# Where the weights' parts and the activations' parts begin in on-chip memory: other offsets, modulo 256 bytes, between the two operands of the large matrix products

## The chip, the cores and the metric

The kernel runs on one core of one Trainium2 chip. Its time is the device time of one execution in microseconds. Three runs of the kernel before took 2641.08, 2643.85 and 2647.0 us; the median, 2643.85 us, is the time that the change is measured against. One further execution was profiled.

## The reference

The reference is two transformer blocks one behind the other on a sequence of 256 tokens of width 1024, all in float32. What matters here are its large products, `x @ W` with 256 rows in `x`:

```python
x = x + 0.5 * swiglu(rms_norm(x, ...), w_gate, w_up, w_down)      # width 2816, twice
u = rms_norm(x, mix_norm) @ w_in ...; x = x + concat([a_out, b_out]) @ w_out
for i in range(2):                                                # two layers
    y = ssd_mixer(hn, ...) if i == 0 else retention(hn, ...)
    h = h + y
    h = h + peer_ffn(rms_norm_2(h, ffn_norm[i]), peer_w_q[i], peer_keys[i], peer_u[i], peer_v[i])
    g = sigmoid(rms_norm_2(h, ple_norm[i]) @ ple_gate[i]); h = h + g * (p[i] @ ple_proj[i])

def peer_ffn(h, w_q, sub_keys, u, v):        # 16384 experts, of which each token uses 8 x 16
    ...                                      # idx, gate: top 16 of the keys' products, per head
    hid = gelu(einsum('tkd,td->tk', u[idx], x))
    return einsum('tk,tkd->td', gate * hid, v[idx])
```

## The kernel before

**Products in parts.** Every large float32 product is made of three products of a reduced type (`fp32r`). The weights `w` and the activations are each split in two parts: the high part is a rounded copy (ScalarE), the low part is what the rounding left (VectorE). `mm3` (L321 to L325) then issues three matrix products into one accumulator: high by high (L323), high by low (L324), low by high (L325). For each of them TensorE first loads a 128x128 stationary operand (PEld in the profile), then streams the moving operand past it (PE).

**Units.** All weights come as 856 units of up to 128 x 1024 floats, in one fixed list (`units`, L1308). The class `Stream` brings them in: `load` starts the DMA of a unit into one of three buffers `w`; `part` makes the parts `wh` (ScalarE, L258) and `wl` (VectorE, L260) in one of three buffers each, and in some stages in one or two lent buffers more; `next` hands a unit's parts to a stage and lets `part` run a few units ahead. A buffer of parts is free again when TensorE has done the last product that reads it. TensorE runs all products in the order in which they are written.

**Two kinds of product.** In nearly all stages the weights' part is the stationary operand and 256 tokens of an activation's part are the moving one (`fm_unit`, L330, and the like): 24 products of 256 columns to a unit. So it is in the two feed-forward blocks, the mixers, the experts' first half, and the gates at the end of each layer. The experts' first half takes 128 units of `peer_u` per layer (in `peer`, L1067), in each of which the inner products of 128 experts with 256 tokens are made; beside them VectorE runs the routing (`route`, side work handed out by `Side.run`, some 1.5 us a unit) and then the building of the gates (`gated`). In the experts' second half, 128 units of `peer_v` per layer, the activation's part (the gated `hid`) is stationary and 512 columns of a weights' part move: 12 products of 512 columns to a unit, with the rest of the gates built beside its first 64 units. The values of the mixers (`w_mv`, `w_uv`, `ret_v`) are also of this second kind.

**Where the operands begin.** The built program gives each buffer a fixed address. Of the two operands of a product, the first byte of each within a partition, modulo 256, is what the change is about:

- All buffers of weights' parts begin at 64 modulo 256, the lent ones too, and pieces of 128 columns lie 512 bytes apart, so every piece of a unit has the same remainder. In the `peer_u` units alone, unit k begins 4 x (k mod 64) bytes further on (`self.ws.at`, L1377; `ROOM` is 64 floats).
- All activations' parts that take part in 256-column products begin at 0 modulo 256.
- In the experts' second half the activations' parts of the experts 4b to 4b+3 begin 4 x (4b mod 64) bytes into their buffer (`part_tiles`, L1167), so at 16b modulo 256, and the weights' parts at 64.

Taken as the activations' remainder less the weights' remainder, modulo 256, this makes

| products | offset before |
|---|---|
| 256 columns, all stages but `peer_u` | 192 |
| 256 columns, `peer_u` unit k | 192 - 4 (k mod 64): each multiple of 4 occurs in two units of each layer |
| 512 columns, experts 4b to 4b+3 | 16b - 64: each multiple of 16 occurs in two groups of four experts in each layer |
| 512 columns, values of the mixers | 192 |

In `peer_u`, unit k = 3 has the offset 180, and k = 5 the offset 172; in the experts' second half the offset is 0 for b = 4 and b = 20.

Of the kernel before, what the change touches and what calls it, by code (L numbers as in the profile page):

```python
# [22 lines left out]
FR = mybir.dt.float32r  # L23
# [8 lines left out]
P = 128  # L32
# [3 lines left out]
KC = D // P  # L36
# [8 lines left out]
PK, PH, PT = 128, 8, 16  # L45
UNIT = 1024
# [169 lines left out]


ROOM = 64


class Stream:
# [3 lines left out]
    def __init__(self, nc, wpool, hpool, units, w_bufs, ahead):  # L225
        self.nc, self.wpool, self.hpool = nc, wpool, hpool
        self.units, self.w_bufs, self.ahead = units, w_bufs, ahead
        self.loaded = self.parted = self.given = 0
        self.w, self.parts = {}, {}
        self.pool_every = 0  # L230
        self.spare, self.spares, self.until = None, 0, 0
        self.at = {}

    def lend(self, pool, n, until):

# [10 lines left out]
    def part(self):  # L246
        if self.parted < len(self.units):
            while self.loaded <= self.parted:
                self.load()
            nc, n = self.nc, self.units[self.parted][1]  # L250
            w = self.w.pop(self.parted)
            lent = self.parted < self.until and self.parted % (3 + self.spares) >= 3
            pool = self.spare if lent else self.hpool
            i = self.at.get(self.parted, 0)
            room = UNIT if lent else UNIT + ROOM
            h = pool.tile([P, room], FR, tag="wh", name="wh")[:, i:i + UNIT]
            l = pool.tile([P, room], FR, tag="wl", name="wl")[:, i:i + UNIT]
            nc.scalar.copy(h[:, :n], w[:, :n])  # L258
            own = self.pool_every and self.parted % self.pool_every == 0
            (nc.gpsimd if own else nc.vector).tensor_tensor(l[:, :n], w[:, :n], h[:, :n].bitcast(FT), OP.subtract)  # L260
            self.parts[self.parted] = (h, l)
            self.parted += 1
            while self.loaded < min(self.parted + self.w_bufs, len(self.units)):
                self.load()
# [46 lines left out]
class Program:  # L311
# [25 lines left out]
    def part_tiles(self, at=0):  # L337

        a = self.xpool.tile([P, 8 * S + ROOM], FR, tag="ah", name="ah")[:, at:at + 8 * S]
        return [a[:, k:k + 4 * S].rearrange("p (c t) -> p c t", c=4) for k in (0, 4 * S)]  # L340
# [299 lines left out]
    def mixer(self, r, ready):  # L640
        nc, ws = self.nc, self.ws
        with ExitStack() as ctx:
# [121 lines left out]
            for d in range(3):  # L764
                for _ in range(3):
                    next(mla, None)
                part(d, 4)
            for _ in mla:
                pass
            for d in range(3):  # L770
                part(d, 0)
                self.residual(d, ps[d], ready)
# [294 lines left out]
    def peer(self, l, r, g, ready):  # L1067
        nc, ws = self.nc, self.ws
        with ExitStack() as ctx:
            pool = ctx.enter_context(self.tc.tile_pool(name="peer", bufs=1))  # L1070
# [56 lines left out]
            for b in range(PK // 2):  # L1127
# [11 lines left out]
                if b == PK // 4:  # L1139
                    side.finish()  # L1140
                    scratch.close()
                    pool = ctx.enter_context(self.tc.tile_pool(name="peer2", bufs=1))
# [17 lines left out]
            for e in range(PK):  # L1160
                b, j = divmod(e, 4)
                if e == PK // 2:
                    side.finish()
                    gates.close()
                    self.lend(ws.given + PK - e, 1, ctx)
                if j == 0:
                    ah, al = self.part_tiles(4 * b % ROOM)  # L1167
                    c = 4 * b % (PK // 2)
                    self.split(ah, al, G[2 * e // PK][:, c:c + 4, :])
                group.append((e, ws.next(UNIT), ah[:, j, :], al[:, j, :]))  # L1170
                if e == PK - 2:
                    continue
                if e == PK - 1:
                    self.new_parts()
                for k in range(2):
                    w = slice(512 * k, 512 * k + 512)
                    for t in range(NT):
                        o = slice(t * P, (t + 1) * P)
                        for i, (wh, wl), h, lo in group:
                            self.mm3(acc[t][k], h[:, o], lo[:, o], wh[:, w], wl[:, w], i == 0, i == PK - 1)  # L1180
                    if e == PK - 1:
                        self.features(acc, k, G[0], ready)
                group = []
                side.run(1.2)
# [123 lines left out]
    def units(self):  # L1308
        def rows(name, lo=0, hi=None):
            ap = self.a[name]  # L1310
            out = []
            for u in range(lo, ap.shape[0] if hi is None else hi):
                n = ap.shape[2]
                out += [(ap[u][:, c:min(c + UNIT, n)], min(UNIT, n - c)) for c in range(0, n, UNIT)]
            return out

        def halves(name):
            u = rows(name)
            out = []
            for d0 in range(0, KC, 4):  # L1320
                some = range(d0, d0 + 4)
                out += [u[2 * d + c] for c in range(2) for d in some]
            return out

        self.peer_at = []
        u = rows("ffn1_gu") + rows("ffn1_dn")
        u += rows("w_in", 0, 8) + rows("w_mv") + rows("w_in", 8) + rows("w_kr") + rows("w_uq") + rows("w_uk") + rows("w_uv")
        u += [(self.a["w_out"][d][:, c:c + 512], 512) for c in (512, 0) for d in range(3)] + rows("w_out", 3)
        u += rows("ffn2_gu") + rows("ffn2_dn")
        for l in range(2):  # L1330
            if l == 0:
                u += rows("ssd_in", 0, 1) + rows("ssd_dt") + rows("ssd_in", 1) + halves("ssd_out")
            else:
                for h in range(RET_H):
                    for n in ("ret_qk", "ret_v", "ret_g"):
                        u += rows(n, 4 * h, 4 * h + 4)
                u += halves("ret_out")
            self.peer_at.append(len(u))
            u += rows(f"peer_q{l}") + rows(f"peer_u{l}") + rows(f"peer_v{l}")
            u += rows(f"ple_p{l}") + rows(f"ple_g{l}")  # L1340
        return u

# [22 lines left out]
    def run(self):  # L1365
        nc, tc = self.nc, self.tc
        with ExitStack() as ctx:
# [6 lines left out]
            self.ps2 = None  # L1374
            ctx.callback(lambda: self.ps2 and self.ps2.close())
            self.ws = Stream(nc, wpool, hpool, self.units(), 3, 2)
            self.ws.at = {n + KC * 2 + k: k % ROOM for n in self.peer_at for k in range(PK)}  # L1377

            self.x = consts.tile([P, KC, S], FT, name="x")
            for c in range(0, KC, 2):  # L1380
# [56 lines left out]
            pool = more.enter_context(tc.tile_pool(name="both", bufs=1))  # L1437
# [17 lines left out]
            for l in range(2):  # L1455
# [18 lines left out]
                if l == 0:  # L1474
                    more = ExitStack()
                    pool = more.enter_context(tc.tile_pool(name="xparts2", bufs=1))
# [47 lines left out]
```

## Time and profile before

| | us |
|---|---|
| median of three runs | 2643.85 |
| the profiled execution, time | 2648.24 |
| its span, from the first to the last instruction | 2646.4 |
| TensorE busy (PE) in it | 2579.6 |
| VectorE busy (DVE) | 2003.2 |
| ScalarE busy (ACT) | 1338.3 |

The profile is of one execution. A matrix product's duration in it is that of one product through a pipeline: products start closer to one another than they last, so that the start of one to the start of the next is what a product costs in a dense stretch. PE is shown as busy from a product's start to its modelled end. "Idle before" is the time in which an engine did nothing just ahead of an instruction, and an arrow names what ended that wait.

In the order of time the stages of TensorE are: first feed-forward block to 197 us, first mixer to 323 us (its first eight units alike, to 220 us), second feed-forward block to 503 us, second mixer (`ssd`) to 716 us, 16 units of routing queries to 762 us, `peer_u` of layer 0 to 1158 us, `peer_v` to 1543 us, the layer's gate to 1572 us, the retention mixer to 1776 us, queries to 1820 us, then `peer_u` (to 2218 us), `peer_v` (to 2603 us) and gate of layer 1.

### The profile page before, as it was taken

To read this page: it belongs to the slowest core of one execution; us is meant where nothing else is said; L and a number is where in the kernel's file an instruction comes from. 1 tells how busy PE (TensorE), PEld (TensorE's weight loads), DVE (VectorE), ACT (ScalarE), POOL (GpSimd) and SP (SyncE) were. 2 spreads that over 40 slices of the span, in tenths; PEclk is the share of its full clock that TensorE was granted. 3 is DMA by queue.
4 is the path that set the end of the run, shared out by engine and by line. 5 is a ranking of instruction groups with operands and counts; after the bars stand their busy time and mean duration, and the time that the engine had idled before them with its cause. 6 is when DMAs were issued, how large, how long until landed. Compare 5 with 4: busy or idle time off the path is not lost.

```text
span 2646.4 us, 49065 instructions
## 1 busy us (share of the span) xinstructions
PE 2579.6 (97%) x19798; PEld 2387.6 (90%) x19798; DVE 2003.2 (76%) x3473; ACT 1338.3 (51%) x1824; POOL 192.5 (7%) x216
## 2 busy tenths in 40 slices
PE   8999999998999999999999989999999999999996
PEld 8998899988999999988788879999999998878886
DVE  8656776689789988868865566668999886886555
ACT  6445655577554443444444465555444344444444
POOL 2000100100102020000000030010212000000002
PEclk9999999999999999999999989999999999999998
DMA  6664366564465655555566555556565555555662
GB/s 219 193 185 141 119 198 189 170 208 144 132 197 170 197 173 161 165 177 171 173 185 191 190 160 176 168 162 193 177 191 176 161 162 176 172 171 187 191 189 94
DMA packets 128037, 460.20 MB, mean 174 GB/s; under 512 B 14688, under 2 KB 15424, under 8 KB 127168
## 3 DMA queue, kind: packets, MB, share of 16 engines
q1 hardware_dynamic: 125984, 452.32, 54.9%
q0 software_dynamic: 1536, 4.20, 0.5%
q8 instruction: 155, 2.54, 0.4%
q10 hardware_dynamic: 288, 0.53, 0.1%
q14 instruction: 74, 0.61, 0.1%
HBM read 455.91 MB, written 1.08 MB: 173 GB/s over the span
## 4 chain that ended last, share of the span: by engine, by line
PE 89%; DVE 7%; ACT 2%; issue 1%; DMA 1%; POOL 0%; POOLq 0%; DVEq 0%; ACTq 0%
PE mm L323 18%; PE mm L324 18%; PE mm L325 18%; PE acc L324 9%; PE acc L323 9%; PE acc L325 9%; PE mm L1119 2%; DVE wl L260 2%; DVE eq L1248 1%; DVE f L1251 1%; PE pv L324 1%; PE pv L325 1%; PE sc L1218 1%; PE pv L323 1%; DVE ca L841 0%
## 5 line engine op out<-in xcount | busy, mean ns | idle before, releaser
L258 ACT CAST wh<-w 128x1024 fp32r<-128x1024 f32 x856 | 889.5, 1041 | 1180.3 <-PE mm L324 579.3
L260 DVE TENSOR_TENSOR wl<-w,wh 128x1024 fp32r<-128x1024 f32 x856 | 1045.9, 1223 | 453.3 <-ACT wh L258 451.5
L323 PE MATMUL mm<-ah,wh 128*128 128x256 f32 x3448 | 976.0, 283 | 22.2 <-DVE cv L837 13.7
L325 PE MATMUL mm<-ah,wl 128*128 128x256 f32 x3448 | 970.9, 282 | 6.4 <-DVE wl L260 6.0
L324 PE MATMUL mm<-ah,wh 128*128 128x256 f32 x3448 | 972.2, 282 | 0.0
L323 PEld LDWEIGHTS mm<-ah,wh 128*128 128x128 f32 x3448 | 653.6, 190 | 25.3 <-issue 7.4
L325 PEld LDWEIGHTS mm<-ah,wl 128*128 128x128 f32 x3448 | 651.5, 189 | 11.0 <-DVE wl L260 9.7
L324 PEld LDWEIGHTS mm<-ah,wh 128*128 128x128 f32 x3448 | 652.5, 189 | 0.8 <-issue 0.3
L324 PE MATMUL acc<-wl,ah 128*128 128x512 f32 x1024 | 406.8, 398 | 0.0
L325 PE MATMUL acc<-wh,ah 128*128 128x512 f32 x1024 | 402.4, 394 | 0.0
L323 PE MATMUL acc<-wh,ah 128*128 128x512 f32 x1024 | 369.9, 395 | 0.0
L323 PEld LDWEIGHTS acc<-wh,ah 128*128 128x128 f32 x1024 | 192.5, 188 | 44.0
L325 PEld LDWEIGHTS acc<-wh,ah 128*128 128x128 f32 x1024 | 192.5, 188 | 42.5
L324 PEld LDWEIGHTS acc<-wl,ah 128*128 128x128 f32 x1024 | 192.7, 188 | 42.0
L373 POOL TENSOR_TENSOR sqa<-sqa,sqt 128x256 f32<-128x256 f32 x82 | 81.9, 998 | 1147.0 <-ACT sqt L372 1020.0
L1123 DVE TENSOR_TENSOR G<-mm,G 128x512 f32<-128x512 f32 x128 | 87.9, 688 | 55.4 <-PE mm L1119 54.9
L323 PE MATMUL mm<-hh,wh 128*128 128x256 f32 x352 | 98.0, 278 | 0.0
L324 PE MATMUL mm<-hl,wh 128*128 128x256 f32 x352 | 98.0, 278 | 0.0
L325 PE MATMUL mm<-hh,wl 128*128 128x256 f32 x352 | 98.0, 278 | 0.0
L1119 PEld LDWEIGHTS <-two 128*128 128x128 f16 x2048 | 69.6, 97 | 21.2 <-issue 16.4
L1107 DVE TENSOR_TENSOR two<-iota,tabs 128x1024 f16<-128x1024 f16 x128 | 87.2, 681 | 0.0
L1119 PE MATMUL mm<-one,two 128*128 128x64 f16 x2048 | 85.8, 194 | 0.0
(348 smaller groups left out, 3225.4 us busy)
## 6 DMA issues: line engine op xcount, KB each, us to landing
w<-in_peer_u_dram SPq DMA_DIRECT2D x256, 512.0 KB, 3.6
w<-in_peer_v_dram SPq DMA_DIRECT2D x256, 512.0 KB, 4.2
w<-in_ffn_gu_dram SPq DMA_DIRECT2D x88, 512.0 KB, 4.3
w<-in_ssd_in_dram SPq DMA_DIRECT2D x40, 512.0 KB, 3.9
w<-in_ffn_dn_dram SPq DMA_DIRECT2D x32, 512.0 KB, 3.6
w<-in_peer_q_dram SPq DMA_DIRECT2D x32, 512.0 KB, 3.8
w<-in_ssd_out_dram SPq DMA_DIRECT2D x16, 512.0 KB, 3.7
w<-in_ple_g_dram SPq DMA_DIRECT2D x16, 512.0 KB, 3.7
```

The lines of the kernel that those rows point to most:

```text
L258: nc.scalar.copy(h[:, :n], w[:, :n])
L260: (nc.gpsimd if own else nc.vector).tensor_tensor(l[:, :n], w[:, :n], h[:, :n].bitcast(FT), OP.subtract)
L323: mm(ps, h, xh, start=start, stop=False, skip_group_check=True)
L324: mm(ps, h, xl, start=False, stop=False, skip_group_check=True)
L325: mm(ps, l, xh, start=False, stop=stop, skip_group_check=True)
L373: (add or nc.gpsimd).tensor_tensor(self.sq[tag], self.sq[tag], t, OP.add)
L1107: nc.vector.tensor_tensor(two, keys.to_broadcast(every), tab[1].to_broadcast(every), OP.is_equal)
L1119: nc.tensor.matmul(ps[:, t, :], two[:, t // 2, :, t % 2], one[i][:, t // 2, :, t % 2], start=i == 0, stop=i == 1)
L1123: nc.vector.tensor_tensor(ga, ps.rearrange("p t e -> p e t"), ga, OP.mult)
L1218: nc.tensor.matmul(ps[:, c * PK:(c + 1) * PK], qT[:, 2 * h + c, t * P:(t + 1) * P], keys[:, c, :], start=True, stop=True)
L1248: nc.vector.tensor_tensor(eq, f[:, c, h, :, None].to_broadcast([P, K, K]), self.iota[:, None, :K].to_broadcast([P, K, K]), OP.is_equal)
L1251: nc.vector.tensor_reduce(f[:, c, h, :], eq, axis=AX.X, op=OP.add)
```

## The change

No instruction is added, taken out or moved on any engine: the order of each engine's instructions and what each waits for are the same, line for line. What changes is where operands begin.

- Every unit's parts begin `ASIDE` = 3 floats into their buffer, at 76 modulo 256, except for the units in the set `wide`, which begin at 64 as before. `wide` holds the `ret_v` and `peer_v` units.
- The `peer_u` units no longer have an offset of their own.
- The activations' parts of the experts' second half all begin 16 floats into their buffer, at 64 modulo 256.
- The lent buffers get the same 64 floats of extra room as the others, 256 bytes more each; other tiles of those stages move by a multiple of 256 bytes.

| products | offset before | offset after |
|---|---|---|
| 256 columns, all stages but `peer_u` | 192 | 180 |
| 256 columns, `peer_u` unit k | 192 - 4 (k mod 64) | 180 |
| 512 columns, `peer_v` | 16b - 64 | 0 |
| 512 columns, `ret_v` | 192 | 192 |
| 512 columns, `w_mv` and `w_uv` (60 products) | 192 | 180 |

```diff
 ROOM = 64
+ASIDE = 3
...
-        self.at = {}
+        self.wide = set()
...
-            i = self.at.get(self.parted, 0)
-            room = UNIT if lent else UNIT + ROOM
-            h = pool.tile([P, room], FR, tag="wh", name="wh")[:, i:i + UNIT]
-            l = pool.tile([P, room], FR, tag="wl", name="wl")[:, i:i + UNIT]
+            i = 0 if self.parted in self.wide else ASIDE
+            h = pool.tile([P, UNIT + ROOM], FR, tag="wh", name="wh")[:, i:i + UNIT]
+            l = pool.tile([P, UNIT + ROOM], FR, tag="wl", name="wl")[:, i:i + UNIT]
...
                 if j == 0:
-                    ah, al = self.part_tiles(4 * b % ROOM)
+                    ah, al = self.part_tiles(16)
...
                     for n in ("ret_qk", "ret_v", "ret_g"):
+                        if n == "ret_v":
+                            self.wide.update(range(len(u), len(u) + 4))
                         u += rows(n, 4 * h, 4 * h + 4)
...
-            u += rows(f"peer_q{l}") + rows(f"peer_u{l}") + rows(f"peer_v{l}")
+            u += rows(f"peer_q{l}") + rows(f"peer_u{l}")
+            self.wide.update(range(len(u), len(u) + PK))
+            u += rows(f"peer_v{l}")
...
-            self.ws.at = {n + KC * 2 + k: k % ROOM for n in self.peer_at for k in range(PK)}
+            self.ws.wide = self.wide
```

## Rows read from the trace of the kernel before

**Rows 1.** The page: span, busy time by engine, and the chain that ended last.
```profile
span 2646.4 us, 49065 instructions
...
PE 2579.6 (97%) x19798; PEld 2387.6 (90%) x19798; DVE 2003.2 (76%) x3473; ACT 1338.3 (51%) x1824; POOL 192.5 (7%) x216
...
PE 89%; DVE 7%; ACT 2%; issue 1%; DMA 1%; POOL 0%; POOLq 0%; DVEq 0%; ACTq 0%
```

**Rows 2.** Busy us (instructions) by stage: PE, PEld, DVE, ACT, POOL; clock, DMA, GB/s.
```profile
36.00:220.00 184.00, 183.84 (x1559) 183.59 (x1558) 127.55 (x171) 92.20 (x132) 11.64 (x11) 1.00 0.64 194
329.00:472.00 143.00, 143.00 (x1262) 142.95 (x1261) 99.30 (x127) 75.03 (x110) 3.69 (x5) 1.00 0.65 194
1730.00:1776.00 46.00, 46.00 (x394) 46.00 (x392) 29.95 (x43) 24.31 (x38) 8.77 (x9) 1.00 0.55 174
```

**Rows 3.** Lines of PE, 36 to 220 us: xcount, busy us, mean ns, idle.
```profile
L325 PE MATMUL mm<-ah,wl 128*128 128x256 f32 x343 | 96.3, 281 | 0.2 <-DVE wl L260 0.2
```

**Rows 4.** Lines of PE, 329 to 472 us.
```profile
L325 PE MATMUL mm<-ah,wl 128*128 128x256 f32 x337 | 93.0, 276 | 0.0
```

**Rows 5.** Timeline of PE in a peer_u unit with k = 5: start, duration (us).
```profile
777.83 0.28 PE L325 MATMUL mm<-nh,wl 128*128 128x256 f32 x1
...
778.55 0.28 PE L325 MATMUL mm<-nh,wl 128*128 128x256 f32 x1
```

**Rows 6.** Timeline of PE in a peer_u unit with k = 3.
```profile
1830.29 0.28 PE L323 MATMUL mm<-nh,wh 128*128 128x256 f32 x1
...
1831.09 0.28 PE L324 MATMUL mm<-nl,wh 128*128 128x256 f32 x1
```

**Rows 7.** Lines of PE in the unit with k = 3, 1829.8 to 1832 us.
```profile
L324 PE MATMUL mm<-nl,wh 128*128 128x256 f32 x7 | 1.9, 277 | 0.0
```

**Rows 8.** Lines of PE in peer_u beside the routing, 865 to 950 us.
```profile
L324 PE MATMUL mm<-ah,wh 128*128 128x256 f32 x231 | 65.3, 283 | 0.0
L325 PE MATMUL mm<-ah,wl 128*128 128x256 f32 x230 | 64.7, 281 | 0.0
```

**Rows 9.** Lines of PE in peer_u beside the gates, 975 to 1124 us.
```profile
L324 PE MATMUL mm<-ah,wh 128*128 128x256 f32 x368 | 103.6, 282 | 0.0
L325 PE MATMUL mm<-ah,wl 128*128 128x256 f32 x368 | 103.4, 281 | 0.0
```

**Rows 10.** Busy us by stage, beside the routing of layer 0.
```profile
820.00:830.00 10.00, 10.00 (x87) 10.00 (x86) 9.29 (x30) 4.41 (x6) 0.00 (x0) 1.00 0.55 168
842.00:861.00 19.00, 17.93 (x145) 17.06 (x143) 19.00 (x30) 7.50 (x9) 12.45 (x13) 1.00 0.52 166
```

**Rows 11.** Lines of PE in the retention mixer, 1600 to 1730 us.
```profile
L325 PE MATMUL mm<-bh,wl 128*128 128x256 f32 x223 | 62.6, 281 | 0.0
```

**Rows 12.** Lines of PE in peer_v without side work, 1355 to 1521 us.
```profile
L325 PE MATMUL acc<-wh,ah 128*128 128x512 f32 x239 | 94.2, 394 | 0.0
```

**Rows 13.** Lines of PE in the peer_v group with b = 20, 1399.6 to 1409.9 us.
```profile
L325 PE MATMUL acc<-wh,ah 128*128 128x512 f32 x16 | 6.2, 389 | 0.0
```

**Rows 14.** Lines of PE in peer_v beside the gates, 1157 to 1355 us.
```profile
L325 PE MATMUL acc<-wh,ah 128*128 128x512 f32 x256 | 100.5, 395 | 0.0
L323 PE MATMUL acc<-wh,ah 128*128 128x512 f32 x258 | 86.7, 397 | 0.0
```

**Rows 15.** Lines of PE in the peer_v group with b = 4, 1206.85 to 1219.05 us.
```profile
L325 PE MATMUL acc<-wh,ah 128*128 128x512 f32 x17 | 6.6, 390 | 0.0
L323 PE MATMUL acc<-wh,ah 128*128 128x512 f32 x16 | 5.8, 396 | 0.0
```

**Rows 16.** Lines of ACT, peer_u (975 to 1124 us), then feed-forward (329 to 472 us).
```profile
L258 ACT CAST wh<-w 128x1024 fp32r<-128x1024 f32 x47 | 49.4, 1050 | 89.7 <-PE mm L324 79.0 <-DVE wl L260 8.4 <-DMA w<-in_peer_u_dram 1.8
...
L258 ACT CAST wh<-w 128x1024 fp32r<-128x1024 f32 (+1 forms) x55 | 56.9, 1035 | 64.3 <-PE mm L324 60.1 <-DMA w<-in_ffn_gu_dram 3.5 <-ACT sqb L369 0.6
```

**Rows 17.** Lines of DVE, peer_u (975 to 1124 us), then feed-forward (329 to 472 us).
```profile
L260 DVE TENSOR_TENSOR wl<-w,wh 128x1024 fp32r<-128x1024 f32 x46 | 56.2, 1221 | 3.8 <-ACT wh L258 3.6
...
L260 DVE TENSOR_TENSOR wl<-w,wh 128x1024 fp32r<-128x1024 f32 (+1 forms) x54 | 64.7, 1201 | 39.2 <-ACT wh L258 39.1
```

More of the change, by code (lines that the diff above doesn't have):

```diff
@@ L1323, in halves @@
             return out
-        self.peer_at = []
+        self.peer_at, self.wide = [], set()
         u = rows("ffn1_gu") + rows("ffn1_dn")
```

## The prediction

> **What bounds the kernel now.** I read the page first: TensorE is busy for 2579.6 of 2646.4 us, and 89% of the chain that ended last is TensorE's [rows 1]. There the reader is to see that little waits for anything but TensorE's own stream, so that the question is how closely its products follow one another. For that I read the stages with the counts of their instructions. All have the granted clock 1.00, the 2.4 GHz level. Two stretches of the same shape and the same offset, 192, have different paces: 36 to 220 us holds 1559 products in 184 us, 118.0 ns each; 329 to 472 us holds 1262 in 143 us, 113.3 ns [rows 2]. VectorE is busy for 69% of either, so neither waits for it. The mean duration of a product differs by the same 5 ns, 281 against 276 [rows 3, 4]; a product's duration less 163 ns is its distance to the next, and I use the means of the lines as a gauge of pace where side work lies between.
>
> Then the experts' first half, where the offset goes through all multiples of 4. At offset 172 six products take 778.55 - 777.83 = 0.72 us, 120 ns each [rows 5]; at 180 seven take 0.80 us, 114 ns [rows 6], with a mean duration of 277 [rows 7]. I followed the start times of all units: the other offsets run at 115 to 125 ns, and three of them, 168, 180 and 204, at 113.3 in all four of their units, whatever went before, a few products after the unit's start or after a break. At 192 a stretch falls after each break into one of the two paces above and stays there. In the experts' second half, twelve 512-column products to a unit, the mean is 394 over all offsets [rows 12] and 389 at offset 0 [rows 13].
>
> So the pace of a dense stretch hangs on the two operands' addresses. The trace before holds both offsets of the kernel after, with the same remainders of both operands (76 and 0 at k = 3; 64 and 64 at b = 4 and 20). Nothing has to be carried over from another shape.
>
> **The change part by part.** No instruction comes, goes or moves, and the waits are the same; each term is a number of products by a difference of pace.
>
> *`peer_u`:* 2 x 128 x 24 = 6144 products. Their lines show 283, 281, 282 and 281 ns [rows 8, 9], mean 281.75, against 277 at 180 [rows 7]: 4.75 ns each, 29.2 us. What is late next is VectorE. Beside the routing it is busy for 9.29 of 10 us, and for 19 of 19 us at the end of each of the two rounds of a layer [rows 10]; there are four such ends, and in them TensorE already waits (17.93 of 19 us). Their 145 or so products each gain nothing, 0.7 us an end, 2.8 us; and ahead of them VectorE goes from 93% to some 97%, so its lead will be used up somewhat earlier. I take off 5 us; the bounds are 0 and the half of the term that lies beside the routing, 14.6. It leaves 24 us.
>
> *First feed-forward block and the mixer's first units:* 1559 products at 113.3 make 176.7 us in place of 184 [rows 2]: 7.3 us. VectorE and ScalarE are at 69% and 50% there, and DMA moves 194 GB/s in either stretch of [rows 2], so the faster one shows that the weights come fast enough.
>
> *Other stretches at the slow pace:* 1730 to 1776 us, 394 products in 46 us, would take 44.6: 1.4 us [rows 2]. The retention mixer's 670 products at 281 [rows 11] would gain 2.7 us if all were slow; side work lengthens some, so 1.5. The first mixer's remaining products and the first layer's queries, some 800, of which I count two thirds: 2.5 us. Together 5.4. The stretches that are at 113.3 now (second feed-forward block, ssd, gates) stay: 0.
>
> *`peer_v`:* 3072 products. Without side work 394 less 389 [rows 12, 13], 5 ns by 1536: 7.7 us. Beside the gates the lines show 395 and 397 over all offsets against 390 and 396 at offset 0 [rows 14, 15]: 5 and 1, so 3 ns by 1536, 4.6 us (bounds 0, if only breaks set the pace there, and 7.7). Together 12.3.
>
> *Parts written 12 bytes off a multiple of 64:* `peer_u` has this already in its units' turn. There the copy takes 1050 ns and the subtraction 1221, against 1035 and 1201 in a stage without, whose means hold shorter units too [rows 16, 17]. At most 15 and 20 ns a unit, and on engines with slack outside the routing: 0. The lent buffers' room moves other tiles by multiples of 256 bytes, which alters no offset: 0. The 60 products of `w_mv` and `w_uv` go from 192 to 180 and are of 512 columns: at most 60 x 8 ns, 0.5 us either way.
>
> The Trainium skill speaks against this in SBUF — State Buffer, section "Door 1: The DMA port swizzle": memory has lines of 16 bytes, and each access that crosses to a new line pays. By that, weights at 76 (12 bytes into a line) would touch 33 lines a load in place of 32 and slow the loads; the trace does not agree, since offset 180 is where a product takes 277 ns and not 281.
>
> Sum: 24 + 7.3 + 5.4 + 12.3 = 49 us. Against the profiled execution's 2648.24 us, 1.8 more than its span, that is 2599. The median of the runs lies 4.4 us lower, and the forecast is against it: 2643.85 - 49 = **2595 us**.
>
> **The rivals.**
> *Two paces at 180 as well.* At 192 the pace is decided anew at each break, so 180 may have a second pace of 118 that four units did not meet. For it: the same addresses give both paces at 192. Against it: in every unit at 180 the products came to 113.3 within seven of a start or a break, also from 118. If half of all stretches were slow, `peer_u` would gain half its 29 less 3 for VectorE, 12; the slow stretches half of 12.7, 6; the some 4,300 products that are fast at 192 now would lose half of 4.5 ns, 10; `peer_v` keeps 12: 20 us, 2624.
> *VectorE takes the gain beside the routing.* With 93% busy now, any unevenness makes TensorE wait. The term of `peer_u` falls to 14.6: 40 us in all, 2604. Against it: TensorE waits nowhere but at the rounds' ends.
> *Nothing.* If the paces followed the time within the program and not the addresses, or if the trace's starts were an artefact, it stays at 2644. The row against it is that 118.0 and 113.3 are whole windows divided by counts [rows 2].
> The Trainium skill's SBUF — State Buffer, section "Who interferes with whom", gives this rival: TensorE has two independent read ports, one for the moving operand and one for the weights' load, and "PE and ACT never wait on anyone". By that rule the offset could not matter and 2644 would stand; 120 against 114 ns at the same shape [rows 5, 6] says that it does here.
> *Slower: long stretches at 180 settle at another pace than short ones.* A unit at 180 is 24 products among others with other offsets; nothing shows 180 kept up over a hundred units. If then the pace were the 120 of offset 172 [rows 5], `peer_u` would lose 6144 x 1.6 = 10 us, the 3300 products that are at 118 now 7 (2 ns each), the 4300 at 113.3 29 (6.7 each), and `peer_v` gain 12: 34 slower, 2678. The point from which it decides: the mean over all 13,700 products is 116.8 now, and 12 us for `peer_v` are 0.9 ns of each, so above 117.7 the kernel is slower.
>
> **How the numbers follow.** Forecast 0.74, two paces 0.12, VectorE 0.07, nothing 0.03, slower 0.04. The forecast's own bounds are all terms whole with nothing off for VectorE and the upper bound beside the gates, 58 us, 2586; and 14.6 off with nothing beside the gates, 35 us, 2609. To leave out no more than 2 in 10 I go to 2582 below and, for the two paces, to 2619 above. A change of under 0.2% (5 us) can't be told from none here. Faster by more: 0.93; within: 0.03; slower: 0.04.
>
> **What would show it.** In the profile after: 36 to 220 us shortened to 177, with the mean of a 256-column product at 276 or 277 in every dense stretch, `peer_u` included, and no more 281; the 512-column means of `peer_v` at 389 without side work; TensorE's waits for VectorE at the four rounds' ends grown by a microsecond or two each; copies and subtractions at 1050 and 1225. Wrong would be: stretches at 281 again (two paces), waits for `wl` all along the routing (VectorE), or means above 281 (slower).

## The result, and the profile after

The kernel after takes 2602.34 us (median of 4 runs, 2600.65 to 2603.25), the kernel before in the same comparison 2645.43 us: ratio 0.9839, 95% interval 0.9822 to 0.9856: faster by 1.6%, clear of noise. The forecast was 2595 us, its range 2582 to 2619.

The page of after, span and busy time by engine [rows 1]:

```profile
span 2598.9 us, 49065 instructions
...
PE 2529.4 (97%) x19798; PEld 2349.1 (90%) x19798; DVE 1999.3 (77%) x3473; ACT 1337.9 (51%) x1824; POOL 192.6 (7%) x216
```

The instructions are as many as before. TensorE's busy time has gone down by 50.2 us, the span by 47.5; the other engines' have hardly moved. So the products themselves have come closer together. By stages (busy us and count of PE, PEld, DVE, ACT, POOL; clock, DMA, GB/s) [rows 2]:

```profile
36.00:213.00 177.00, 177.00 (x1561) 176.91 (x1561) 126.42 (x171) 91.50 (x132) 12.47 (x11) 1.00 0.66 202
329.00:472.00 143.00, 143.00 (x1264) 143.00 (x1263) 96.43 (x125) 74.61 (x110) 5.21 (x6) 1.00 0.64 196
1709.00:1754.00 45.00, 45.00 (x377) 44.95 (x376) 28.54 (x41) 22.24 (x36) 8.16 (x9) 1.00 0.52 158
```

The first stretch has 113.4 ns a product in place of 118.0, the second is at 113.1 as good as unchanged (113.3 before), and the third, the retention's output projection, is slower than before: 119.4 ns against 116.8. The granted clock is 1.00, the 2.4 GHz level, in all of them.

Lines of PE (xcount, busy us, mean ns, idle), 36 to 213 us [rows 3], then `peer_u` beside the gates, 959 to 1104 us [rows 9], then `peer_v` without side work, 1332 to 1512 us [rows 12], and beside the gates, 1140 to 1328 us [rows 14]:

```profile
L325 PE MATMUL mm<-ah,wl 128*128 128x256 f32 x344 | 94.9, 276 | 0.0
```
```profile
L324 PE MATMUL mm<-ah,wh 128*128 128x256 f32 x368 | 102.5, 278 | 0.0
L325 PE MATMUL mm<-ah,wl 128*128 128x256 f32 x367 | 101.9, 278 | 0.0
```
```profile
L325 PE MATMUL acc<-wh,ah 128*128 128x512 f32 x255 | 99.0, 389 | 0.0
```
```profile
L325 PE MATMUL acc<-wh,ah 128*128 128x512 f32 x251 | 97.8, 391 | 0.0
L323 PE MATMUL acc<-wh,ah 128*128 128x512 f32 x250 | 83.0, 392 | 0.0
```

276 is the mean that the fast stretch of before had [rows 4], 389 that of its short example at offset 0 [rows 13]. In `peer_u` the mean is 278, not the 277 of the short example at 180 [rows 7]: some units there are slow. The timeline of PE (start, duration) shows one unit of that stage, k = 79, from its second product to its last, and then the next but one, from its first product to its last:

```profile
985.82 0.28 PE L324 MATMUL mm<-ah,wh 128*128 128x256 f32 x1
...
988.46 0.28 PE L325 MATMUL mm<-ah,wl 128*128 128x256 f32 x1
...
991.89 0.28 PE L323 MATMUL mm<-ah,wh 128*128 128x256 f32 x1
...
994.49 0.28 PE L325 MATMUL mm<-ah,wl 128*128 128x256 f32 x1
```

The first has 22 distances in 2.64 us, 120.0 ns; the second 23 in 2.60 us, 113.0 ns. Both have the same offset and the same shapes. Of the 13,456 distances between 256-column products that follow one another directly, 11,407 are 113 or 114 ns and 1,257 are 119 to 121 (1,082 of them 120); before, 4,292 and 2,379 were, and 4,781 were 117 or 118. Of the 112 units from k = 72 on, where the gates are built beside them, 26 run at 120 ns: the same 13 in either layer, from k = 79 to 116, mostly every third. The trace shows how they come about. The products of the gates come between units in groups of 16 small ones. All 48 units without any other product ahead keep the pace of the unit before; behind a group, 26 of 34 fast streams turn slow, and all 26 slow ones turn fast again.

Since the order is the same, each product is found in both traces, and a stage's length is the distance between the same two products:

| stage, us | before | after | change | predicted |
|---|---|---|---|---|
| first feed-forward, mixer's first units (36 to 220) | 184.6 | 177.4 | -7.2 | -7.3 |
| `peer_u`, both layers | 794.2 | 773.3 | -20.9 | -24 |
| `peer_v`, both layers | 769.7 | 756.1 | -13.6 | -12.3 |
| all else | | | -5.6 | -5.4 |

### The profile page after: what moved, and what is told of

Its sections match the earlier page's. It is cut to its first block, busy times and chain, and to the rows that moved or that the text cites. A ratio compares the mean times of both kernels' runs of the same rounds, so it can differ in the third digit from the quotient of the medians.

```text
span 2598.9 us, 49065 instructions
## 1 busy us (share of the span) xinstructions
PE 2529.4 (97%) x19798; PEld 2349.1 (90%) x19798; DVE 1999.3 (77%) x3473; ACT 1337.9 (51%) x1824; POOL 192.6 (7%) x216
## 4 chain that ended last, share of the span: by engine, by line
PE 77%; DVE 6%; ACT 2%; issue 1%; POOL 0%; DMA 0%; POOLq 0%; DVEq 0%; ACTq 0%
PE mm L323 15%; PE mm L324 14%; PE mm L325 14%; PE acc L324 9%; PE acc L323 9%; PE acc L325 9%; PE mm L1119 2%; DVE wl L260 2%; DVE eq L1248 1%; DVE f L1251 1%; PE pv L324 1%; PE pv L325 1%; PE pv L323 1%; PE sc L1218 1%; DVE ca L841 1%
## 5 line engine op out<-in xcount | busy, mean ns | idle before, releaser
L323 PE MATMUL mm<-ah,wh 128*128 128x256 f32 x3448 | 963.7, 280 | 21.2 <-DVE cv L837 12.4
L325 PE MATMUL mm<-ah,wl 128*128 128x256 f32 x3448 | 959.4, 278 | 9.3 <-DVE wl L260 9.2
L324 PE MATMUL mm<-ah,wh 128*128 128x256 f32 x3448 | 960.5, 279 | 0.5 <-DVE ah L360 0.4
L325 PE MATMUL acc<-wh,ah 128*128 128x512 f32 x1024 | 398.3, 390 | 0.0
L323 PE MATMUL acc<-wh,ah 128*128 128x512 f32 x1024 | 365.1, 391 | 0.0
```

The source lines that it names most:

```text
L323: mm(ps, h, xh, start=start, stop=False, skip_group_check=True)
L324: mm(ps, h, xl, start=False, stop=False, skip_group_check=True)
L325: mm(ps, l, xh, start=False, stop=stop, skip_group_check=True)
```

## The experiments

All 256-column products of one kernel have the same pair of addresses unless the text says otherwise; "moved" products are the 10,344 whose activations lie in the general buffers (`ah`). Addresses are modulo 256, "stage A" is 36 to 135 us of before (the dense part of the first feed-forward block), and `peer_u` is each layer's length. Products whose activations lie in other buffers keep these at 0 in every kernel, so their offset follows from the weights alone. Each row's stage times are from one profiled execution. The rows come from several chips; each ratio is to before on the same one, where before's median lies between 2645.43 and 2646.18 us throughout. The edits shown are cuts against after, but for the second of the next two, which is against before.

| kernel | weights, activations | offset | median us (ratio, interval) | `peer_u`, us | stage A, us |
|---|---|---|---|---|---|
| before (profile) | 64, 0; `peer_u` all | 192 | 2645.43 | 396.8, 397.4 | 99.0 |
| after | 76, 0 | 180 | 2602.34 (0.9839, 0.9822 to 0.9856) | 386.5, 386.8 | 95.0 |
| only_256 | 76, 0 | 180 | 2616.08 (0.9887, 0.9864 to 0.9910) | 386.7, 387.1 | 95.4 |
| only_512 | as before | 192 | 2629.92 (0.9940, 0.9921 to 0.9960) | 396.8, 397.4 | 95.7 |
| acts_moved | 64, 244 | 180 | 2660.73 (1.0059, 1.0036 to 1.0083) | 400.7, 402.7 | 100.4 |
| acts_far | 76, 224 | 148 | 2649.83 (1.0018, 1.0004 to 1.0033) | 400.0, 401.3 | 100.4 |
| both_64 | 140, 64 | 180 | 2617.45 (0.9894, 0.9879 to 0.9910) | 387.1, 387.9 | 100.4 |
| both_back | 44, 224 | 180 | 2609.55 (0.9857, 0.9842 to 0.9872) | 384.6, 385.6 | 95.0 |
| acts_240 | 60, 240 | 180 | 2656.56 (1.0035, 1.0017 to 1.0053) | 397.8, 400.4 | 100.4 |
| off_204 | 52, 0 | 204 | 2623.07 (0.9910, 0.9896 to 0.9923) | 392.6, 394.3 | 99.2 |
| off_168 | 88, 0 | 168 | 2616.05 (0.9880, 0.9865 to 0.9895) | 387.6, 388.7 | 100.4 |
| alt_units | 76 and 88, 0 | 180, 168 | 2601.42 (0.9820, 0.9791 to 0.9849) | 385.4, 386.5 | 95.0 |
| combo | 76, 0; 44, 224; 88, 0 | 180, 168 | 2595.48 (0.9808, 0.9784 to 0.9833) | 383.7, 384.8 | 95.0 |
| after_again | 76, 0 | 180 | 2602.55 (0.9835, 0.9810 to 0.9859) | 386.6, 387.7 | 95.0 |

**The two parts apart.** One kernel has the change without `peer_v`'s part, the other that part alone:

```diff
-                    ah, al = self.part_tiles(16)
+                    ah, al = self.part_tiles(4 * b % ROOM)
```
```diff
-                    ah, al = self.part_tiles(4 * b % ROOM)
+                    ah, al = self.part_tiles(16)
```

> The change without its part in the experts' second half: `peer_v` keeps its offsets 16b - 64, all 256-column products have offset 180. Theory A (each product's pace hangs on its own two addresses, so the two parts add up): the `peer_v` stretches are as long as before (196.3, 188.1, 196.3 and 189.0 us in layers 0 and 1), the rest is as after; the traces of before and after differ there by 13.6 us, so the time is about 2602 + 13.6 = 2616 us. Rival B (`peer_v` gained only because `peer_u`'s weights in front of it, or the buffers' layout, changed): `peer_v` keeps its gain and the time is about 2602 us.

> The kernel before with one edit: the activations' parts of the experts' second half begin 16 floats into their buffer, which makes the offset of all `peer_v` products 0. All else as before. Theory A (parts add up): 2645 - 13.6 = about 2632 us, with `peer_v` stretches of 193.5, 184, 193.5 and 185 us and everything else as before. Rival B (the gain of `peer_v` needs the other part): about 2645 us.

Lines of `peer_v` without side work, 1337 to 1517 us of only_256, then 1348 to 1528 us of only_512:

```profile
L325 PE MATMUL acc<-wh,ah 128*128 128x512 f32 x255 | 100.3, 394 | 0.0
```
```profile
L325 PE MATMUL acc<-wh,ah 128*128 128x512 f32 x255 | 99.0, 389 | 0.0
```

`peer_v` has its old lengths in the one (196.3, 188.1, 196.3, 189.0 us) and its new ones in the other (193.5, 184.1, 193.4, 185.1), and the time of the first is the expected 2616. Theory A holds: the parts add up. But the second missed one expectation. Its program is that of before up to 1158 us, operands' addresses included, and yet stage A ran at the fast pace (36 to 126 us):

```profile
36.00:126.00 90.00, 89.48 (x789) 89.28 (x788) 71.52 (x106) 49.63 (x75) 5.33 (x4) 1.00 0.65 208
```

That is 789 products in 90 us, 114.1 ns, where before had 118.0 [rows 2]. So at 192 the pace of this stretch can differ between two executions (which may have run on different chips), a draw; `peer_u` in contrast repeats to 0.1 us in every piece. The whole times fit this: on one chip nine runs of before spread over 16.3 us (2638.92 to 2655.24), five of after over 1.6 (2601.57 to 2603.12); on another, nine of before over 4.2 alone.

**Which address counts.** The offset 180 made by the activations in place of the weights, and the offset 148 beside weights that stay where after has them:

```diff
-ASIDE = 3
+ASIDE = 0
...
-    def part_tiles(self, at=0):
+    def part_tiles(self, at=61):
```
```diff
-    def part_tiles(self, at=0):
+    def part_tiles(self, at=56):
```

> The same offset by the other operand: all weights' parts go back to 64 modulo 256, and the activations' parts of most stages (10,344 of the 256-column products: `peer_u`, the feed-forward blocks, queries, `ssd` in part) begin at 244 in place of 0, which is 180 again. The remaining 256-column products (mixers, retention) return to 192. `peer_v` stays at 0. Theory A (the difference of the two addresses sets the pace): the moved products run at 113.3 ns with a second pace of 120 in some stretches, as after, `peer_u` takes about 386 us a layer, and the whole lies within some 8 us of after, 2595 to 2610 us. Rival B (it is the weights' own address, 76 against 64, that does it): the 256-column products run as before, `peer_u` at the pace of 192, a mixture of 113.3 and 117.8 ns, and the first feed-forward block at 118; with the gain of `peer_v` alone about 2625 to 2632 us.

> Weights' parts as after (76 modulo 256), the activations' parts of most stages (10,344 of the 256-column products) at 224 in place of 0: offset 148 in place of 180. `peer_v` stays at 0. Theory A (the difference of the two addresses sets the pace): offset 148 ran at 119 to 125 ns in the four `peer_u` units that had it before, 9 ns above the 114.2 that the products average after; 10,344 x 9 = 93 us slower than after, about 2695 us (2660 to 2725 by the ends 119 and 125, less what waits hide). Rival B (the weights' own address does it, the activations' does not matter): as after, about 2602 us.

Both theories fail for the first: it is 58 us above after, and slower than before. In the second the moved products run at 120 ns, so the activations' address does matter and rival B is out; the loss is 47 us and not 93. 120 ns is the low end of what was expected: 6 ns by 10,344 products make 62 us. The rest is hidden where TensorE waited before: its waits for VectorE at L837 fell from 12.4 to 7.9 us, those for `wl` from 9.2 to 5.1. A pair of its own for each operand was the next test: both moved from after's by +64, by -32, and later by -16.

```diff
-ASIDE = 3
+ASIDE = 19
...
-    def part_tiles(self, at=0):
+    def part_tiles(self, at=16):
```

(59 and 56 for -32; 63 and 60 for -16.)

> Both operands of most 256-column products (10,344) moved 64 bytes up together from where after has them: weights' parts at 140, activations' parts at 64 modulo 256, offset 180 as after. `peer_v` as after. What is to be told apart is why offset 180 was slow (120 to 123 ns) when it was made by activations at 244. Theory C (the difference decides as long as the activations begin on a multiple of 64 bytes): the moved products run as after, 113.3 ns with 120 in some stretches, about 2602 us, first feed-forward block 36 to 135 us at 113.3. Rival D (the activations have to begin at 0 modulo 256, wherever the weights are): the moved products run at 120 ns, about 2650 us as with the activations at 224.

> The same with 32 bytes down: weights' parts at 44, activations' parts at 224, offset 180 as after. Beside the earlier run with activations at 224 and weights at 76 (offset 148) only the weights' address differs, beside after both differ. Theory E (only the difference of the two addresses matters, and activations at 244 were slow for being off a multiple of 16 or 32): about 2602 us. Theory C (multiples of 64) and rival D (0 modulo 256): the moved products at about 120 ns, about 2650 us.

> Offset 180 a third time: activations' parts of most stages at 240 and weights' parts at 60, modulo 256. With activations at 224 and weights at 44 this offset kept its pace of 113.3 ns in `peer_u`, with activations at 244 and weights at 64 it did not (120 to 123 ns). Theory I (activations may begin on any multiple of 16 bytes, the difference decides): `peer_u` 384 to 388 us a layer, the whole 2600 to 2618 us, as the other pairs with this offset. Rival J (they must begin on a multiple of 32): the moved products at 120 to 123 ns as with 244, 2650 to 2660 us.

Lines of `peer_u` beside the gates, a window of 143 us in each: both_64, both_back, acts_far, acts_240, acts_moved.

```profile
L325 PE MATMUL mm<-ah,wl 128*128 128x256 f32 x362 | 100.7, 278 | 0.0
```
```profile
L325 PE MATMUL mm<-ah,wl 128*128 128x256 f32 x366 | 101.2, 276 | 0.0
```
```profile
L325 PE MATMUL mm<-ah,wl 128*128 128x256 f32 x350 | 98.8, 282 | 0.0
```
```profile
L325 PE MATMUL mm<-ah,wl 128*128 128x256 f32 x350 | 99.6, 284 | 0.0
```
```profile
L325 PE MATMUL mm<-ah,wl 128*128 128x256 f32 x348 | 99.0, 285 | 0.0
```

With activations at 224 the offset 180 gives 276 and the offset 148 gives 282; with weights at 76 the activations at 0 give 278 and those at 224 give 282. So neither address decides alone. At offset 180 the pairs moved together by 0, +64 and -32 are fast (278, 278, 276), those moved by -16 and -12 are not (284, 285). In `peer_u`, then, the pace hangs on the difference and on where the pair lies within 32 bytes; theories C and D, and I, are out, and E and J hold for that stage. Moving by 16 leaves both remainders of 16 as they were and is slow, so these are not what counts. Whether it is the activations' or the weights' remainder of 32 can't be told from these, since at a fixed difference the two go together. The whole times of these kernels say less, for two reasons. First, their products with other activations got the offsets 116 (both_64), 212 (both_back) and 196 (acts_240): the 2.5 us that both_64 lost in the second feed-forward block are theirs, at 120 ns, while the moved products there run at 113.3. Second, both_64's moved products lost 5 us in stage A to 120 ns, and nearly all of those in the layers' gates run at 120 too. From one trace each a draw as in only_512 can't be excluded; that moving by 64 is harmless outside `peer_u` is not shown.

**Does another offset lack the slow pace?**

```diff
-ASIDE = 3
+ASIDE = 61
```

(6 for the offset 168.)

> After with the weights' parts at 52 modulo 256 in place of 76, activations at 0: offset 204 for the 256-column products. In the kernel before this offset ran at 113.3 ns in all its four `peer_u` units. Theory A (204 is as good as 180): within 3 us of after, with a second pace of its own in some stretches. Theory F (the second pace of 120 ns belongs to the address 76 of the weights and not to the stretches after breaks): the about 1,085 products at 120 ns go to 113.3, 7 us less than after, about 2595 us. Rival G (204 has a second pace in more stretches): up to 2640 us.

> After with the weights' parts at 88 modulo 256, activations at 0: offset 168. It too ran at 113.3 ns in all its four `peer_u` units before. Theory A: within 3 us of after. Theory F: 7 us less than after, about 2595 us. Rival G: up to 2640 us.

Rival G: both are slower than after, by 21 and 14 us. Both have paces of their own beside 113.3: at 168 most units beside the gates repeat distances of 115 to 118 ns (mean 116.7), at 204 about half of the units of `peer_u` run at 120. What four units of each had shown before did not carry over to a hundred in a row; for 180 it carried over for the most part. In the one stretch where after is slower than before, the retention's projection, 168 is fast: 346 products in 39 us, 113 ns (1720 to 1759 us of off_168):

```profile
1720.00:1759.00 39.00, 39.00 (x346) 39.00 (x346) 27.01 (x40) 21.01 (x33) 5.91 (x6) 1.00 0.55 182
```

**Two offsets in turn.**

```diff
-            i = 0 if self.parted in self.wide else ASIDE
+            i = 0 if self.parted in self.wide else ASIDE << self.parted % 2
```

> After with one edit: the parts of every second unit of 256-column products begin 6 floats into their buffer in place of 3, so that offsets 180 and 168 take turns from unit to unit (activations stay at 0, `peer_v` as after). It asks whether a stretch that has fallen into the pace of 120 ns stays there because nothing disturbs it. Theory H (a change of address starts the choice anew, and most choices come to 113.3, as in the four units of each offset in the kernel before, whose neighbours all had other offsets): the slow runs of 11 to 13 units beside the gates go, 975 to 1124 us take about 143.6 us in place of 145.4, the retention's last stretch 44.5 in place of 46.4, and the whole about 2595 us. Rival K (the pace is carried from unit to unit, or each alternation costs a slow start): no gain or a loss, 2602 to 2625 us.

The time is that of after within the measurement, as rival K had it. From k = 72 on (both layers) only 4 of the 56 units at 180 run at 120 ns, where after had 26 of 112; but 28 of the 56 at 168 run at 116.7. So theory H holds in that few units at 180 fall to 120 ns behind units at 168, and it fails in that the gain is given back by the other offset: the stretch that took 975 to 1124 us before takes 144.8 us in place of 145.4, not 143.6. Lines of `peer_u`, 961 to 1104 us:

```profile
L325 PE MATMUL mm<-ah,wl 128*128 128x256 f32 x364 | 101.0, 277 | 0.0
```

**The best pair by stretch.** From its ninth unit on `peer_u` takes 44 and 224, and the retention's projection weights at 88:

```diff
+                self.begin.update({len(u) + k: 6 for k in range(16)})
                 u += halves("ret_out")
...
+            self.begin.update({len(u) - PK + k: 59 for k in range(8, PK)})
...
-                    self.new_parts()
+                    self.new_parts(56)
                     for to, part in ((self.xh, nh), (self.xl, nl)):
```

> After with two stretches changed, from what the runs so far showed. (1) `peer_u` from its ninth unit on takes weights at 44 and activations at 224 modulo 256 in place of 76 and 0: offset 180 as before, but in the run with this pair no unit beside the gates fell to 120 ns (975 to 1124 us took 143.6 us, after 145.4). (2) The weights of the retention's output projection begin at 88, offset 168, where that stretch took 44.4 us in place of 46.4. Theory A (a stretch's pace is settled by its own pair of addresses and its breaks, so that the best pair can be picked stretch by stretch): gains of 2.9 us (layer 0), about 2 (layer 1) and 2 (projection), about 7 us, 2595 us, 0.3% below after on the same chip. Rival L (which pace a stretch falls into hangs on what ran before it, so the gains do not carry over): 2598 to 2606 us, not to be told from after.

> The kernel after once more on the same chip, to compare the last version with: 2602 us, with 36 to 135 us at 113.3 ns and the same units at 120 ns as in its first trace, if the paces are settled by the program; other stretches at 120 ns if they are drawn anew in each execution.

Windows of combo, 36 to 126 us, then `peer_u` beside the gates:

```profile
36.00:126.00 90.00, 90.00 (x796) 90.00 (x795) 71.51 (x107) 49.09 (x75) 5.33 (x4) 1.00 0.67 210
955.00:1098.00 143.00, 143.00 (x1596) 141.81 (x1595) 122.94 (x196) 60.46 (x70) 0.00 (x0) 1.00 0.52 172
```

The same two of after in its second profile:

```profile
36.00:126.00 90.00, 90.00 (x796) 90.00 (x796) 71.69 (x107) 48.97 (x74) 4.58 (x4) 1.00 0.67 210
958.00:1101.00 143.00, 143.00 (x1564) 141.71 (x1563) 122.14 (x196) 59.16 (x69) 0.00 (x0) 1.00 0.51 167
```

Theory A holds. The version takes 2595.48 us (2592.43 to 2596.84, 5 runs), after on the same chip 2602.55 (2601.57 to 2603.12): 7.1 us less, and the ranges don't touch. In the 143 us beside the gates 1596 matrix products fit in place of 1564, no unit beside the gates is at 120 ns, and of the 13,456 distances 293 are 119 to 121 ns in place of 1,407. By the traces the two `peer_u` stages gained 3.0 and 2.8 us over after's second one, and the projection 2.1, as expected; `ssd` is 2.2 us shorter and the last gate 1.4 longer, neither of which the edit touches. Of after's second trace the feed-forward blocks and the retention repeat the first to 0.2 us, but beside the gates 35 units in place of 26 are at 120 ns. From k = 79 on they are the same 26, in only_256 as well; the others lie at k = 70 to 76, so that only the first ones beside the gates are drawn anew.

## Why the prediction was right, and where it missed

**The mechanism** was right: a dense stretch's pace hangs on the two operands' addresses, and most of a gain read off a few units before came true over all units.

**The forecast** was some 7.5 us too low, and only 1.4 of that is in the sum: 49 us against 47.6 between the two profiled executions (2648.24 and 2600.65 us). 4.4 are the step from the profiled execution of before to the median: the prediction took a gain read in a longer execution off the time of a shorter one. Part of what makes an execution of before long can be the draw seen in only_512, and that the change takes away; the medians differ by 43.1 us. The last 1.7 are after's median above its own profiled execution.

**`peer_u`** was put at 24 us and gave 20.9. The gross 29.2 is about right (below); what is taken off was mis-sized. 5 us were for VectorE. The waits of PE (us in total, times, longest) say how much it was, for after:

```profile
PE mm L325 <- DVE wl L260: 9.2, 20, 1.0
```

and for before:

```profile
PE mm L325 <- DVE wl L260: 6.0, 11, 1.0
```

That is 3.2 us more in the whole kernel. 2.6 of it are in `peer_u` (8.0 us for 5.4), at the rounds' ends, as the prediction placed it; at one of them 17.19 of 19 us are busy now, with VectorE at 19.00 [rows 10]:

```profile
828.00:847.00 19.00, 17.19 (x140) 16.01 (x138) 19.00 (x30) 7.11 (x9) 12.46 (x13) 1.00 0.54 168
```

What the prediction's likeliest case left out is the second pace. 26 units beside the gates and 5 beside the routing, 24 products each, by 6.7 ns are 5.0 us. 29.2 - 2.6 - 5.0 = 21.6, 0.7 more than was measured. Combo, without those units, gains 25.7, and its waits for `wl` are 2.8 us longer than before's (8.8 for 6.0): 28.5 of the gross 29.2.

So the step that failed, though the forecast held, is the argument against the first rival, "in every unit at 180 the products came to 113.3 within seven of a start or a break". That rested on four units; 180 has a second pace, which a unit keeps to its end. It is 120 ns and not 118, and 1,082 of 13,456 distances have it and not half, so it costs some 7 us and not 29. That it costs so little could not be read from before: 168 and 204, as spotless there, lost 14 and 21 us against after. To that extent the choice of 180 was lucky.

**First feed-forward block and mixer's first units:** 7.2 us for 7.3. But only_512 shows that part of this was the draw of the execution that was profiled: at 192 the stretch has come at 118 and at 114. At 180 with weights at 76 it was at 113.3 in all four traces with that pair throughout or in this stretch (after, after_again, only_256, combo). What the change gains there on the average over executions is thus less than 7 us, by an amount that no run here tells.

**Other stretches:** 5.6 for 5.4, but not from where it was expected: `ssd` gave 2.2 us, the first layer's queries 1.3, the rest of the first mixer 1.1, the retention 2.1; in this is a loss of 0.5 in its projection, which the prediction had gaining 1.4. The second feed-forward block and the first gate are 1.3 us longer.

**`peer_v`:** 13.6 for 12.3. Without side work 7.9 for 7.7; beside the gates 5.7 for 4.6, within its bounds.

**Parts 12 bytes off:** nothing, as forecast. Lines of ACT and DVE, 959 to 1104 us of after [rows 16, 17]:

```profile
L260 DVE TENSOR_TENSOR wl<-w,wh 128x1024 fp32r<-128x1024 f32 x46 | 56.1, 1220 | 3.7 <-ACT wh L258 3.5
L258 ACT CAST wh<-w 128x1024 fp32r<-128x1024 f32 x47 | 49.3, 1049 | 85.8 <-PE mm L324 83.5 <-DMA w<-in_peer_u_dram 2.4
```

The rival that nothing happens is out. The Trainium skill, SBUF — State Buffer, section "Who interferes with whom", gives TensorE independent read ports for the moving operand and the weights' load, and says that PE never waits on anyone. The traces do not agree with what the prediction drew from it, that the offset can't matter: here only addresses were changed, and a unit takes 113.3 or 120 ns a product.

## What to carry to other kernels

Where TensorE is busy all the time, divide dense windows by their product counts, stage by stage: two paces of one shape can point at the operands' addresses, and a few floats of room at a buffer's start are a cheap trial. Keep both remainders of a good pair. Moving both by -32 or +64 bytes kept the pace in `peer_u`; in stage A +64 did not, in the one trace taken. Before such a gain is promised for a hundred units in a row, try it for a hundred in a row: four examples of an offset between other offsets told little of 168 and 204.

## What the runs showed of the hardware

- The products of 256 columns show a few stable, repeating paces: 113.3 ns (272 cycles of 2.4 GHz), 117.8, 120.0 (288), and 116.7 at offset 168. Beside the gates one is taken up behind a group of small products and kept until the next (all 48 units with nothing ahead, from k = 72 on in after, have the pace of the unit before). The same pair can have two: 76 and 0 changes from 113.3 to 120 at one group and back at the next.
- The choice repeats from execution to execution in `peer_u` with offsets in turn (0.1 us a piece between before and only_512) and with 76 and 0 from k = 79 on (the same 26 slow units in after, after_again and only_256). It differs between executions at k = 70 to 76, and in stage A at 192 (99.0 and 95.7 us).
- The pair of addresses counts by its difference and by its place within 32 bytes: moving both by 12 or 16 bytes loses what 180 gains, moving both by -32 or +64 keeps it in `peer_u`.
- The Trainium skill's page TensorE: Matmul & The Clock Gate, section "Wait — 56ns, not 53.3ns?", has columns / 2.4 GHz plus a floor of 2.5 ns from one product to the next; worked out for 256 columns that is an estimate of 109.2 ns. No stretch here comes to it; the fastest is 113.3 in over 10,000 products of combo.

Which part of the chip makes the addresses count stays open: the runs moved addresses alone, and changed neither the shape of the loads nor their order.
